# Ten seven-product units dealt evenly among the query/key tiles, with linear attention moved into the middle of the first stage

## The chip, the cores and the metric

The kernel runs on one core of a Trainium2 chip. The metric is the device time of one execution in microseconds (us), as a median over runs. Three runs of the kernel before gave 1986.81 us (1984.18 to 1990.47). The profile is of one further execution, which took 1983.73 us; its span, from the first to the last instruction, is 1981.9 us, so 1.83 us lie outside the span.

## The reference, cut to what matters

One layer of a hybrid model on 256 tokens of width 2048, all in float32. The input is multiplied by one wide matrix, and its product is cut into parts:

```python
parts = jnp.split(x @ w_in, cuts, axis=-1)      # 3 x (q, k, v) of 1024, gq, gk, gv, gr, g_low, m_a, m_b
# 3 groups of dilated attention, 8 heads of 128; mixed by a softmax over their log sums
ya = ya @ w_proj_a
log_a = log_sigmoid(g_low @ gla_gate_w + gla_gate_b) / 16
o = _gla(gq / 16, gk, gv, log_a)                # linear attention, 4 heads of 256 keys and 512 values
o = o * rsqrt(mean(o * o) + eps) * gla_norm_g
yb = (o * silu(gr)) @ w_proj_b
y = sigmoid(m_a) * ya + sigmoid(m_b) * yb
x = layernorm(alpha * x + y @ w_out)
x = layernorm(alpha * x + conv_ffn(x))          # 5632 wide, gated, with a 3-tap convolution
```

## The kernel before

**Two-part products.** Every weight is read once, in pieces of 128 x 2048 floats (1 MB). `split` (L135) makes of a piece a rounded high part on ScalarE (ACT, tile `whi`, L136) and the remainder on VectorE (DVE, tile `wlo`, L137), and TensorE (PE) multiplies high by high, high by low and low by high in a format that it takes at one pass. There are three buffers for `whi` and two for `wlo`. Raw pieces have buffers of two kinds: `raw`, two of them, and `quarter`, six. SyncE (SP) issues the loads in order of its queue; a load waits until a split has freed its buffer.

**Stage one** makes all that is multiplied out of `x`, in three shapes of work.

- A *tile* (`b16`, L219) is one piece with 128 output columns: 16 matmuls of 512 columns with `whi` (L212) and 16 of 256 columns with `wlo` (L214). 16 tiles make the linear attention's keys and queries (`gkq`, L501), and 48 make queries and keys of the 8 heads (`head`, L522).
- A *unit* (`seven`, L294) makes 1024 output columns by a seven-product scheme over quarters of the matrix, called A11 to A22 and B11 to B22 as usual: 8 loads into `quarter` buffers, and 7 products of 2 parts with 12 matmuls of 512 columns each (24 a product, L308). Its steps are `p1, p5, p67(0), p67(1), p3, p4, p2`. The products A, D, B, E take as weights sums of quarters: some are added by DVE (`add`, L321), others by a DMA that accumulates into the other quarter (`add_by_dma`, L324), which GpSimd (POOL) issues. `p67` adds `B22` into `T` by DVE and into `B12` by DMA; `p4` adds `B21` into `T` by DMA. The x side needs four sums of quarters of x, from `combine` (L273). 11 units are made: 3 for the heads' values (`v`), 4 for the output gates (`m`), 2 for the linear attention's values (`gv`), 2 for its gate (`gr`).
- *Side work* is a list of closures, `side`, from which `pump` (L173) takes one after each step and each tile: for each head a bias, three score blocks, two softmaxes, three transposes and three value products (`attend`, L421).

The order of the work (L554 to L577) is: two tiles, `combine`, and then the 63 steps of nine units (v, m, gv) with one tile after nearly every step. When the tiles are used up the low-rank gate input is made (L581 to L615), then the two `gr` units run with two closures after each step, among them `gate, decay, keys, att` and `outs` of the four heads of linear attention (`gla`, L624). Within a head these are a chain: a gate product (`pz`, L633) on PE, ACT functions and a running sum on DVE, decayed keys (`xk`, L652 to L684) on DVE, the products `patt` (L692) on PE, a mask on POOL (L700), and the products `pgo` (L710, L712) on PE. `drain()` (L730) makes the rest, and the pool `early` is closed. A scheduler orders the instructions of each engine, within what the buffers allow; the order of a program below is what it made.

**The other stages.** The heads' sums are loaded and split (L762 to L765) and multiplied by `w_proj_a` (`yp`, L792 to L798) while `gated_out` makes `ob`; then come `w_proj_b` (`pb`), `w_out` (`wo`), a layer norm, and the feed-forward part (`fg`, `fu`, `wd`). They use plain chunks (`a_chunk`, L248): for 512 output columns and 16 row blocks, four pieces with 24 matmuls of 512 columns each (L244 to L246). Their pieces come through the two `raw` buffers.

Of the kernel before, what the change touches and what calls it, by code (L numbers as in the profile page):

```python
# [17 lines left out]
P = 128  # L18
# [39 lines left out]
def hybrid_layer(ctx: ExitStack, tc: tile.TileContext, wp, xt, wgl, gw, par, relb, onehot, rows, xk, out):  # L58
# [80 lines left out]
    def raw_tile(i, tag="raw", bufs=2):  # L139
        return wpool.tile([P, 2048], F32, tag=tag, name=f"{tag}_{i}", bufs=bufs)  # L140
# [30 lines left out]
    side = []  # L171

    def pump(n=1):  # L173
        for _ in range(n):
            if side:
                side.pop(0)()

    def drain():
        while side:
            side.pop(0)()  # L180
# [92 lines left out]
    def combine(xs, raw):  # L273

        out = [res(f"comb{i}") for i in range(4)]
        for j in range(4):
# [11 lines left out]
        return out  # L288
# [5 lines left out]
    def seven(name, xs, comb, i, store):  # L294
# [48 lines left out]
        def p67(p):  # L343
            def f():
# [7 lines left out]
                add_by_dma(st["B12"][p], b)  # L352
# [68 lines left out]
    def attend(h, qk):  # L421
# [70 lines left out]
        return bias, [scores(g) for g in range(3)], [soft(0), soft(1), turn(0), turn(1), values, mix(0), turn(2), mix(1), mix(2)]  # L492
# [6 lines left out]
    tiles = []  # L499

# [13 lines left out]

    for which in range(2):
        for h in range(GH):
            f = gkq(which, h)
            first = not tiles
            tiles.append(f(0, [pair_of_x(j) for j in range(4)] if first else (None,)))
            tiles.append(f(1))  # L520
# [20 lines left out]
    for h in range(NH):  # L541
        tiles.extend(head(h))

# [10 lines left out]
    with tc.issue_after(loaded.ins):  # L554
        tiles.pop(0)()
    comb = []
    tiles.pop(0)()
    comb.extend(combine(X, XR))
    steps = []
    for g in range(3):  # L560
        steps.extend(seven("v", X, comb, AT["v", g], to_v(g)))
    for u in range(4):
        steps.extend(seven("m", X, comb, AT["m", u], to(M[u // 2], u % 2)))
    for u in range(2):
        steps.extend(seven("gv", X, comb, AT["gv", u], to(GV, u)))
    late = []
    for u in range(2):
        late.extend(seven("gr", X, comb, AT["gr", u], to(GR, u)))
    ratio = len(tiles) / len(steps)
    done = 0  # L570
    for n, step in enumerate(steps):
        step()
        pump()
        while done < (n + 1) * ratio and tiles:
            tiles.pop(0)()
            done += 1
            pump()  # L577

    glr = tmp("glr")  # L581
    nc.gpsimd.dma_start(glr, wgl)
    glh = tmp("glh", F32R)
    gll = tmp("gll", F32R)
    split(glh, gll, glr)


    places = [slice(r, r + RANK) for r in (0, 32, 64)]
    stack = slice(0, 64 + RANK)
    gws = []  # L590
    for j in range(2):
        w = blk("gws")
        nc.gpsimd.memset(w[stack], 0.0)
        for r in places:
            nc.gpsimd.dma_start(w[r], gw[:, j * 512 : (j + 1) * 512])
        gws.append(blk("gwp", F32R))
        nc.scalar.activation(gws[j][stack], w[stack], AF.Copy)
        r = places[1]
        nc.vector.tensor_tensor(gws[j][r], w[r], gws[j][r].bitcast(F32), op=ALU.subtract)
    gl = tmp("gl")  # L600
    nc.gpsimd.memset(gl[stack], 0.0)
    pg = bank("pgl")
    for kc in range(16):
        w = slice(kc * RANK, (kc + 1) * RANK)
        xo = xop(kc)
        nc.tensor.matmul(pg[:RANK], glh[:, w], xo, start=(kc == 0), stop=False)
        nc.tensor.matmul(pg[:RANK, S:], gll[:, w], xo[:, :S], start=False, stop=(kc == 15))
    nc.scalar.activation(gl[:RANK], pg[:RANK, :S], AF.Copy)
    nc.vector.tensor_tensor(gl[:RANK], pg[:RANK, S:], gl[:RANK], op=ALU.add)
    for r in places[1:]:  # L610
        nc.sync.dma_start(gl[r], gl[:RANK])
    glp = tmp("glp", F32R)
    nc.scalar.activation(glp[stack], gl[stack], AF.Copy)
    r = places[2]
    nc.vector.tensor_tensor(glp[r], gl[r], glp[r].bitcast(F32), op=ALU.subtract)  # L615

    O = [[] for _ in range(GH)]
    rmask = blk("rmask")
    nc.gpsimd.memset(rmask, 1.0)
    nc.gpsimd.memset(rmask.rearrange("p (c t) -> p c t", t=CH)[:, :, 0:1], 0.0)  # L620
    NG = blk("ng")
    nc.gpsimd.dma_start(NG, rows[4:5, :512].to_broadcast([P, 512]))

    def gla(h):  # L624
        st = {}

        def gate():
            pz = bank("pz")
            z = blk("gz")
            for j in range(2):  # L630
                dt = 2 * h + j
                c = slice(j * S, (j + 1) * S)
                nc.tensor.matmul(pz[:, c], gws[h // 2][stack, (dt % 4) * P : (dt % 4 + 1) * P], glp[stack], start=True, stop=True)  # L633
# [7 lines left out]
            nc.vector.tensor_tensor_scan(c, rmask, z, 0.0, op0=ALU.mult, op1=ALU.add)  # L641
            st["c"] = c

        def decay():
            c = st["c"]
# [59 lines left out]
        def outs():  # L705
            a = st["a"]
            gv = [fetch("gv", d) for d in GV[h]]
            for t in range(2):
# [10 lines left out]
                nc.vector.scalar_tensor_tensor(o, po, rs, NG, op0=ALU.mult, op1=ALU.mult)  # L719
                O[h].append(spill("os", o))  # L720

        return [gate, decay, keys, att], outs

    for h in range(GH):
        stages, o = gla(h)
        side.extend([*stages, o])
    for step in late:
        step()
        pump(2)
# [349 lines left out]
```

## Time and profile before

| | |
|---|---|
| median of 3 runs | 1986.81 us (1984.18 to 1990.47) |
| profiled execution | 1983.73 us, span 1981.9 us |
| PE busy | 1859.2 us, 94% of the span |
| DVE busy | 1333.7 us, 67% |
| ACT busy | 974.6 us, 49% |
| HBM read | 372.18 MB, 198 GB/s over the span |

How to read what the prediction quotes: the page's slices cut the span in 40 equal parts of 49.5 us, and each digit is the busy share in tenths; PEclk is the clock that TensorE was granted, in tenths of full speed. In rows by windows each engine has its busy time and, as (x...), the number of instructions, and then come the clock, the share of DMA engines that were busy and GB/s. In rows of the timeline the first two numbers are the start and the time in us; xN is how many instructions of a kind follow one another; in brackets stands the idle time of the engine before the row and what released it. In rows of the chain of waits there are the start, the time and what took it. In groups by line "a<-b" is output and input, xN the count, and after the bar come busy us and mean ns of one, then idle us before them.

### The profile page before, as it was taken

How to read it: one execution, taken by the hardware profiler on the slowest of the kernel's cores; microseconds unless marked ns; L12 is line 12 of the kernel's file. 1: busy time of each engine (PE TensorE's matmuls, PEld its weight loads, DVE VectorE, ACT ScalarE, POOL GpSimd, SP SyncE). 2: the span in 40 equal slices, each digit the busy share in tenths (PEclk: the TensorE clock that was granted, in tenths of full speed). 3: DMA queues.
4: the chain of work that ended last, by engine and by line, in shares of the span. 5: the costliest groups of instructions: out<-in, count | busy, mean ns of one | idle time of the engine just before them, and what ended most of it. 6: DMA issues, size and time to landing. Idle time of an engine off the chain costs nothing.

```text
span 1981.9 us, 23097 instructions
## 1 busy us (share of the span) xinstructions
PE 1859.2 (94%) x9246; PEld 1558.7 (79%) x9246; DVE 1333.7 (67%) x1181; ACT 974.6 (49%) x951; POOL 203.2 (10%) x305
## 2 busy tenths in 40 slices
PE   6889999999999999785699998899999999999996
PEld 4768888888888888663478886788888888888885
DVE  7667887878888788685375556766545666446657
ACT  5355555555546555465453334454434555335442
POOL 0100101110110111112320002400000000000001
PEclk9989999999999999887699999999999999999998
DMA  8689888887988978674386554555555555565553
GB/s 311 219 255 292 254 306 243 270 287 225 313 226 270 295 234 291 196 212 135 128 288 226 196 191 147 206 187 188 191 194 191 187 187 189 195 229 193 192 191 126
DMA packets 71927, 438.77 MB, mean 221 GB/s; under 512 B 9873, under 2 KB 10796, under 8 KB 24844
## 3 DMA queue, kind: packets, MB, share of 16 engines
q1 hardware_dynamic: 50316, 345.10, 47.9%
q0 software_dynamic: 21360, 91.95, 18.9%
q8 instruction: 72, 1.18, 0.2%
q14 instruction: 35, 0.29, 0.0%
q10 hardware_dynamic: 144, 0.26, 0.0%
HBM read 372.18 MB, written 20.09 MB: 198 GB/s over the span
## 4 chain that ended last, share of the span: by engine, by line
PE 82%; DMA 6%; DVE 6%; issue 3%; ACT 2%; POOL 1%; SPq 0%; ACTq 0%; POOLq 0%; DVEq 0%
PE qk L212 8%; PE fu L212 8%; PE fg L212 8%; PE qk L214 4%; PE fu L214 4%; PE fg L214 4%; PE wd_t L244 4%; PE wd_t L246 4%; PE wd_t L245 4%; DMA quarter<-quarter 3%; PE mA L308 2%; PE gqk L212 2%; DVE wlo L137 2%; PE mD L308 2%; PE mE L308 2%
## 5 line engine op out<-in xcount | busy, mean ns | idle before, releaser
L136 ACT ACTIVATE whi<-raw 128x2048 fp32r<-128x2048 f32 (+1 forms) x239 | 452.7, 1894 | 502.1 <-DMA raw<-in_wp 381.3
L137 DVE TENSOR_TENSOR wlo<-raw,whi 128x2048 fp32r<-128x2048 f32 (+1 forms) x239 | 544.7, 2279 | 213.2 <-PE wd_t L245 52.3
L137 DVE TENSOR_TENSOR wlo<-quarter,whi 128x2048 fp32r<-128x2048 f32 x154 | 351.8, 2287 | 151.5 <-ACT whi L136 125.2
L136 ACT ACTIVATE whi<-quarter 128x2048 fp32r<-128x2048 f32 x154 | 294.2, 1917 | 233.3 <-DMA quarter<-quarter 79.2
L212 PE MATMUL qk<-x,whi 128*128 128x512 f32 x768 | 188.6, 396 | 0.0
L212 PE MATMUL fu<-x,whi 128*128 128x512 f32 x688 | 166.1, 394 | 6.0 <-DVE yb L237 6.0
L212 PEld LDWEIGHTS qk<-x,whi 128*128 128x128 f32 x768 | 142.1, 188 | 28.5
L212 PE MATMUL fg<-x,whi 128*128 128x512 f32 x672 | 160.3, 391 | 2.0 <-ACT whi L136 2.0
L212 PEld LDWEIGHTS fu<-x,whi 128*128 128x128 f32 x688 | 127.6, 190 | 31.0 <-DVE yb L237 6.2
L212 PEld LDWEIGHTS fg<-x,whi 128*128 128x128 f32 x672 | 123.7, 188 | 26.3 <-ACT whi L136 2.2
L244 PE MATMUL wd_t<-whi,h 128*128 128x512 f32 x352 | 137.1, 390 | 0.0
L245 PE MATMUL wd_t<-wlo,h 128*128 128x512 f32 x352 | 137.0, 389 | 0.0
L246 PE MATMUL wd_t<-whi,h 128*128 128x512 f32 x352 | 136.9, 389 | 0.0
L214 PEld LDWEIGHTS qk<-x,wlo 128*128 128x128 f32 x768 | 98.6, 191 | 3.8
L321 DVE TENSOR_TENSOR quarter<-quarter,quarter 128x2048 f32<-128x2048 f32 x44 | 100.4, 2286 | 0.7
L214 PE MATMUL qk<-x,wlo 128*128 128x256 f32 x768 | 100.0, 283 | 0.0
L214 PEld LDWEIGHTS fu<-x,wlo 128*128 128x128 f32 x688 | 88.2, 191 | 3.3
L214 PE MATMUL fu<-x,wlo 128*128 128x256 f32 x688 | 89.2, 283 | 0.0
L214 PEld LDWEIGHTS fg<-x,wlo 128*128 128x128 f32 x672 | 86.2, 191 | 3.3
L214 PE MATMUL fg<-x,wlo 128*128 128x256 f32 x672 | 87.2, 283 | 0.0
L246 PEld LDWEIGHTS wd_t<-whi,h 128*128 128x128 f32 x352 | 66.1, 188 | 14.0 <-DVE h L137 0.2
L244 PEld LDWEIGHTS wd_t<-whi,h 128*128 128x128 f32 x352 | 66.1, 188 | 13.8 <-ACT h L136 0.5
(313 smaller groups left out, 2768.9 us busy)
## 6 DMA issues: line engine op xcount, KB each, us to landing
raw<-in_wp SPq DMA_DIRECT2D x235, 1024.0 KB, 5.0
quarter<-in_wp SPq DMA_DIRECT2D x88, 1024.0 KB, 7.2
quarter<-quarter POOLq DMA_DIRECT2D x44, 1024.0 KB, 8.5
sp<-c POOLq DMA_DIRECT2D x16, 256.0 KB, 4.1
m<-sp POOLq DMA_DIRECT2D x16, 256.0 KB, 5.3
row<-in_rows POOLq DMA_DIRECT2D x16, 256.0 KB, 3.9
bias<-bvd POOLq DMA_DIRECT2D x32, 96.0 KB, 9.8
v<-vs POOLq DMA_DIRECT2D x24, 128.0 KB, 8.5
```

Of the source, the lines that this page charges most:

```text
L136: nc.scalar.activation(hi, src, AF.Copy)
L137: nc.vector.tensor_tensor(lo, src, hi.bitcast(F32), op=ALU.subtract)
L212: nc.tensor.matmul(ps, parts(kc)[0], opnd(kc), start=(kc == 0), stop=False)
L214: nc.tensor.matmul(ps[:, S:], parts(kc)[1], opnd(kc)[:, :S], start=False, stop=(kc == nk - 1))
L244: nc.tensor.matmul(ps, xh, hi, start=first, stop=False)
L245: nc.tensor.matmul(ps, xh, lo, start=False, stop=False)
L246: nc.tensor.matmul(ps, xl, hi, start=False, stop=last)
L308: nc.tensor.matmul(ps, a(kc)[which], w[:, k * 512 : (k + 1) * 512], start=(first and w is hi and which == 0 and kc == 0), stop=(w is lo an ...
L321: tt(a, a, b, op=ALU.add)
```

## The change

1. **Start.** Four tiles come first instead of two, and `combine` is cut in four parts, of which two are called ahead of the third tile and two ahead of the fourth. The first unit (`v`, 0) makes all its sums by DVE (`by_dma=False`): four more 128 x 2048 additions on DVE, and four accumulating DMAs fewer.
2. **Ten units instead of eleven.** `m` has three units. The last 1024 columns of its second gate are two plain chunks (`a_chunk`, 8 pieces), at the end of stage one, with three closures after each piece.
3. **The order.** The steps of all ten units (v, gv, gr, m; 74 entries with four marks) and the rest of the tiles (65 entries) are dealt out evenly, so about six tiles stand among seven steps, and the units of `gr` no longer come last.
4. **Linear attention in the middle.** The low-rank part, the mask, the four gates and the norm's gain are put on the side list once the `gkq` tiles are done. Each head's running sum is written to DRAM and fetched again by `decay` (two DMAs of 256 KB more for each head, on POOL's queue). The stages `decay, keys, att, outs` of a head follow a head of dilated attention (after heads 1, 2, 3 and 4). A closure may carry a mark ("values", "gv"), and `pump` stops in front of it until the units that it needs are done.
5. **The end of stage one.** The splits of the heads' sums (`ya_parts`) are closures that run during the two plain chunks.
6. **Buffers.** From the end of stage one on, pieces are loaded into the six `quarter` buffers instead of the two `raw` buffers.

```diff
+    home = ["raw", 2]
+    def raw_tile(i, tag=None, bufs=None):
+        tag, bufs = (tag, bufs) if tag else home
...
     def pump(n=1):
         for _ in range(n):
             if side:
-                side.pop(0)()
+                mark, f = side[0] if isinstance(side[0], tuple) else (None, side[0])
+                if mark and mark not in passed:
+                    return
+                side.pop(0)
+                f()
...
-                add_by_dma(st["B12"][p], b)
+                (add_by_dma if by_dma else add)(st["B12"][p], b)
...
-                add_by_dma(a, b)
+                (add_by_dma if by_dma else add)(a, b)
...
-            st["c"] = c
+            DEC[h] = spill("gcs", c)
         def decay():
-            c = st["c"]
+            c = fetch("gc", DEC[h])
...
+    def head_tiles():
+        for h in range(NH):
+            yield from head(h)
+            if h in (1, 2, 3, 4):
+                yield lambda h=h: side.extend(gla_stages[h - 1])
+    def of_tiles():
+        yield from gkq_tiles()
+        yield lambda: side.extend([low_rank, start_mask, *gla_gates, norm_gain])
+        yield from head_tiles()
+    def by_unit(name, n, sink, mark=None):
+        for u in range(n):
+            yield from seven(name, X, comb, AT[name, u], sink(u), by_dma=(name, u) != ("v", 0))
+        yield lambda: passed.add(mark)
+    tiles = of_tiles()
+    with tc.issue_after(loaded.ins):
+        next(tiles)()
+    next(tiles)()
+    comb, part = combine(X, XR)
+    part(0)
+    part(1)
+    next(tiles)()
+    part(2)
+    part(3)
+    next(tiles)()
+    def of_units():
+        yield from by_unit("v", 3, to_v, "values")
+        yield from by_unit("gv", 2, lambda u: to(GV, u), "gv")
+        yield from by_unit("gr", 2, lambda u: to(GR, u))
+        yield from by_unit("m", 3, lambda u: to(M[u // 2], u % 2))
+    units = list(of_units())
+    rest = list(tiles)
+    done = 0
+    for n, step in enumerate(units):
         step()
-        pump(2)
+        pump()
+        while done < (n + 1) * len(rest) / len(units):
+            rest[done]()
+            done += 1
+            pump(2 if len(side) > 8 else 1)
+    side.extend(ya_parts(h) for h in range(NH))
+    for n in range(2):
+        pss = a_chunk("m", xop, 16, AT["mb"] + 4 * n, 3)
+        for t in range(2):
+            c = blk("mc")
+            nc.scalar.activation(c, pss[t], AF.Copy)
+            M[1][2 + n][t] = spill("ms", c)
     drain()
+    home[:] = "quarter", 6
```

Three places show what the scheduler made of it.

The first is VectorE at the start (`raw` and `quarter` are raw pieces, `comb` the sums of quarters of x, `gqk` the result of a tile). In the program before, the splits of the first unit's quarters stand directly behind the split of the second tile (`raw_196`), with the sums of `combine` around them:

```order
L137 TENSOR_TENSOR wlo_199<-raw_196,whi_198 128x2048
L237 TENSOR_TENSOR gqk_192<-gqk_159,pa_193 128x256
L137 TENSOR_TENSOR wlo_314<-quarter_308,whi_313 128x2048
L281 TENSOR_TENSOR comb_244<-xraw_115,xraw_137 128x256
L137 TENSOR_TENSOR wlo_330<-quarter_310,whi_329 128x2048
L237 TENSOR_TENSOR gqk_192<-gqk_202,pa_235 128x256
L282 TENSOR_TENSOR comb_245<-comb_244,xraw_115 128x256
```

In the changed program the third tile's split (`raw_276`) and then `combine` stand there:

```order
L137 TENSOR_TENSOR wlo_199<-raw_196,whi_198 128x2048
L246 TENSOR_TENSOR gqk_192<-gqk_159,pa_193 128x256
L137 TENSOR_TENSOR wlo_279<-raw_276,whi_278 128x2048
L291 TENSOR_TENSOR comb_244<-xraw_115,xraw_137 128x256
L246 TENSOR_TENSOR gqk_192<-gqk_202,pa_235 128x256
L292 TENSOR_TENSOR comb_245<-comb_244,xraw_115 128x256
```

So two more tiles come ahead of the first unit. Within that unit VectorE has more to do. Before, one addition of quarters stands at each half of `p67`, and none for `B12`; now there are two, the second of them for `B12` (`quarter_487`), here at `p67(0)`:

```order
L137 TENSOR_TENSOR wlo_534<-raw_531,whi_533 128x2048
L332 TENSOR_TENSOR quarter_395<-quarter_395,quarter_578 128x2048
L332 TENSOR_TENSOR quarter_487<-quarter_487,quarter_578 128x2048
L137 TENSOR_TENSOR wlo_582<-quarter_395,whi_581 128x2048
L246 TENSOR_TENSOR gqk_478<-gqk_537,pa_570 128x256
L137 TENSOR_TENSOR wlo_599<-quarter_487,whi_598 128x2048
```

Both additions stand ahead of the two splits of that step.

The second place is TensorE at the end of stage one. In the program before, the last heads of linear attention stand there alone (`pz` the gate, `patt` the decayed keys by the queries, `pgo` the result), and the first matmul of the next stage, `yp_t`, comes behind them:

```order
L633 MATMUL pz_6806<-glp_5936,gwp_5894 128x256 x2
L692 MATMUL patt_6844<-gq_6826,xk_6831 128x64 x4
L692 MATMUL patt_6844<-qx_6841,xk_6831 128x128 x2
L692 MATMUL patt_6844<-gq_6826,xk_6832 128x64 x4
L710 MATMUL pgo_6862<-gv_6858,att_6855 128x512
L710 MATMUL pgo_6874<-gv_6858,att_6855 128x512
L712 MATMUL pgo_6874<-gv_6860,att_6855 128x512
L244 MATMUL yp_t_864_6937<-whi_6941,ya_6897 128x512
```

In the changed program `patt` of the first such head stands within a query/key tile (`qk_3151`), with a product of a unit behind it:

```order
L223 MATMUL qk_3151<-x_85,wlo_3148 128x256 x3
L223 MATMUL qk_3151<-x_86,wlo_3148 128x256
L676 MATMUL patt_3131<-qx_3093,xk_3083 128x128 x2
L676 MATMUL patt_3131<-gq_3078,xk_3084 128x64 x4
L223 MATMUL qk_3151<-x_86,wlo_3148 128x256 x3
L319 MATMUL gvE_2940<-whi_3193,x_85 128x512 x8
```

And the first matmul of the next stage follows the last of the plain chunks (`m_t`):

```order
L255 MATMUL m_t_851_6784<-whi_6890,x_86 128x512
L253 MATMUL m_t_852_6785<-whi_6890,x_86 128x512
L254 MATMUL m_t_852_6785<-wlo_6891,x_86 128x512
L255 MATMUL m_t_852_6785<-whi_6890,x_86 128x512
L253 MATMUL yp_t_866_6942<-whi_6946,ya_6599 128x512
L254 MATMUL yp_t_866_6942<-wlo_6947,ya_6599 128x512
```

What stood alone on TensorE now has tiles and products on both sides.

The third place is TensorE between `p67(1)` and `p4` of the second `gv` unit. Before, a tile (`qk_5610`), the product `gvD` and a second tile (`qk_5700`) lie between the two; the rows are the end of the first tile, the product, two transposes and the beginning of the second tile:

```order
L214 MATMUL qk_5610<-x_86,wlo_5607 128x256 x4
L308 MATMUL gvD_5376<-whi_5653,comb_27_243 128x512 x8
L308 MATMUL gvD_5376<-wlo_5654,comb_27_243 128x512 x4
L308 MATMUL gvD_5376<-whi_5669,comb_27_243 128x512 x8
L308 MATMUL gvD_5376<-wlo_5670,comb_27_243 128x512 x4
L463 MATMUL ppt_5688<-ident,s_600_5456 128x128
L466 MATMUL ppt_5688<-ident,s_601_5457 128x128 x2
L212 MATMUL qk_5700<-x_83,whi_5696 128x512 x4
```

In the changed program the product stands inside the only tile (`qk_3151`), and the product of `p4`, `gvE` out of `x_85`, is the last row of the piece with `patt` above:

```order
L221 MATMUL qk_3151<-x_86,whi_3147 128x512 x4
L319 MATMUL gvD_2856<-whi_3096,comb_27_243 128x512 x8
L319 MATMUL gvD_2856<-wlo_3097,comb_27_243 128x512 x4
L319 MATMUL gvD_2856<-whi_3112,comb_27_243 128x512 x8
L319 MATMUL gvD_2856<-wlo_3113,comb_27_243 128x512 x4
L223 MATMUL qk_3151<-x_83,wlo_3148 128x256 x4
L223 MATMUL qk_3151<-x_84,wlo_3148 128x256 x2
```

So one tile fewer stands between the two steps in this unit. The same holds for the first `gr` unit; the other units keep two tiles there.

More of the change, by code (lines that the diff above doesn't have):

```diff
@@ L275, in combine, with part @@
         out = [res(f"comb{i}") for i in range(4)]
-        for j in range(4):
+        def part(j):
             n_blk[0] += 1
@@ L513, in gkq @@
         return f
[L515 to L520, printed above, removed]
     def head(h):
@@ L552, in to @@
         return f
[L554 to L611, printed above, removed]
```

104 lines of the change are left out of this document (73 added, 31 removed).

## The prediction

> **What bounds the kernel now.** I read the page first, then the chain of waits, then a table of busy time by windows whose edges I took from TensorE's timeline: its first tile, the end of the first unit, the last tile and product that are fed in rhythm, and the first matmul of the next stage. The page:
>
> ```profile
> span 1981.9 us, 23097 instructions
> ...
> PE 1859.2 (94%) x9246; PEld 1558.7 (79%) x9246; DVE 1333.7 (67%) x1181; ACT 974.6 (49%) x951; POOL 203.2 (10%) x305
> ...
> PE   6889999999999999785699998899999999999996
> ...
> PEclk9989999999999999887699999999999999999998
> ```
>
> PE is the bound nearly everywhere; slices 0 to 2 and 16 to 19 are the weak places, and there the clock drops too. The windows:
>
> ```profile
> 10.15:122.69 112.54, 86.82 (x403) 69.98 (x404) 77.67 (x81) 54.91 (x55) 9.25 (x14) 0.89 0.79 262
> 122.69:794.88 672.19, 671.45 (x3450) 569.46 (x3448) 537.92 (x390) 375.69 (x304) 89.60 (x137) 1.00 0.86 270
> 794.88:979.75 184.87, 127.19 (x460) 93.61 (x458) 110.40 (x110) 89.25 (x124) 35.64 (x59) 0.77 0.53 158
> 979.75:1982.00 1002.25, 971.02 (x4936) 825.26 (x4936) 606.22 (x598) 451.54 (x466) 67.16 (x87) 0.99 0.56 196
> ```
>
> From 122.69 to 794.88 PE idles 0.7 of 672 us at full clock, though DVE is busy 80% and the DMA engines 86%. So where tiles and products alternate, PE alone sets the pace, and the chain of waits gives that pace:
>
> ```profile
> 122.85 5.47 PE vA L308 x24
> 128.32 3.63 PE gqk L212 x16
> 133.86 5.47 PE vA L308 x24
> ```
>
> A product (24 matmuls) takes 5.47 us. From one product to the next with a tile between are 11.01 us, so a tile (32 matmuls) takes 5.54. The counts fit: 8 tiles and 6 products are 400 of the 403 matmuls in the first window.
>
> With these two prices, the first window holds 8 x 5.54 + 6 x 5.47 = 77.1 us of PE work and takes 112.5: **35.4 us are lost**. The third holds 13 products and little else, busy 127.19 us at clock 0.77, which is 97.9 us of full-clock work; it takes 184.87: **87.0 us are lost**. This is what the loss there looks like, in the list of waits and in PE's timeline:
>
> ```profile
> PE patt L692 <- DVE xk L668: 19.6, 3, 10.2
> PE pgo L710 <- POOL att L700: 5.6, 3, 3.4
> ...
> 941.51 1.97 PE L692 MATMUL patt<-gq,xk 128*128 128x64 f32 x8 [10.22 <-DVE xk L668]
> ...
> 961.39 1.97 PE L692 MATMUL patt<-gq,xk 128*128 128x64 f32 x8 [6.72 <-DVE xk L668]
> ...
> 979.75 0.80 PE L244 MATMUL yp_t<-whi,ya 128*128 128x512 f32 x1 [8.42 <-ACT ya L136]
> ```
>
> The chain of a head runs over five engines, and PE has nothing else to do; last it waits for the first split of the heads' sums. Now the start:
>
> ```profile
> 10.15 5.23 PE L212 MATMUL gqk<-x,whi 128*128 128x512 f32 x12 [4.28 <-ACT whi L136]
> ...
> 20.54 3.92 PE L212 MATMUL gqk<-x,whi 128*128 128x512 f32 x16 [0.69 <-ACT whi L136]
> ...
> 28.95 1.98 PE L308 MATMUL vA<-whi,x 128*128 128x512 f32 x8
> ...
> 44.05 3.78 PE L308 MATMUL vD<-whi,comb 128*128 128x512 f32 x8 [4.72 <-ACT whi L136]
> ...
> 107.19 3.79 PE L308 MATMUL vE<-whi,x 128*128 128x512 f32 x8 [14.65 <-ACT whi L136]
> ...
> 91.42 20.81 DMA quarter<-quarter
> ...
> 36.00:60.00 24.00, 16.82 (x79) 13.51 (x79) 24.00 (x27) 11.43 (x14) 1.79 (x2) 0.86 0.87 247
> ```
>
> The hole of 14.65 us ends an accumulating DMA of 20.81 us (`p4`), the one of 4.72 us follows `combine` on a DVE that is busy without a gap from 36 to 60. After both, eight matmuls took 3.78 us instead of 1.98: half clock.
>
> **The change, part by part.** The sum is made against the profiled execution, 1983.73 us.
>
> *Linear attention and the end of stage one: -87.0 us.* The PE work of the third window stays and is done elsewhere: the `gr` products in the rhythm of the second window, `patt` and `pgo` between tiles. The splits of the heads' sums lie under the plain chunks, so the wait of 8.42 us goes with the rest. What is late next is priced under new waits.
>
> *Start: 35.4 us lost become 13, -22.4 us.* DVE's prices are these, and a sum or split of `combine` is a quarter of the last row:
>
> ```profile
> L137 DVE TENSOR_TENSOR wlo<-quarter,whi 128x2048 fp32r<-128x2048 f32 x154 | 351.8, 2287 | 151.5 <-ACT whi L136 125.2
> ...
> L321 DVE TENSOR_TENSOR quarter<-quarter,quarter 128x2048 f32<-128x2048 f32 x44 | 100.4, 2286 | 0.7
> ...
> 38.04 1.41 DVE L137 TENSOR_TENSOR comb<-comb,comb 128x256 fp32r<-128x256 f32 x4
> ```
>
> The first tile takes 9.7 us (10.15 to its last matmul, with the loads of x), 4.2 over its price, and the second waits 0.7 as now. From 20.5 on DVE has to make 5 large splits (near 2.25 us each back to back), 25 pieces of `combine` and 3 small additions (0.35 each) up to the last split of `p1`: 21 us, to 41.5. PE comes to that split after three tiles and three quarters of a product, at 41.3. So `combine` is covered by the two tiles put ahead. From there to the second `p67` DVE has the rest of `combine`, 9 splits and 6 additions: 39 us, to 80.5. PE has 35 us of tiles and products in that time: it waits about 5. Together 4.2 + 0.7 + 5 = 10, and 3 for half clock behind the waits. The DMA hole of 14.65 us is gone, since the four DMAs of this unit are additions of 2.29 us. Bounds: 5 (no wait on DVE) and 35.4 (as now).
>
> Here a rule speaks against the edit. The Trainium skill ("Perfetto Trace Analysis", Optimizing Scalar/DVE Operations) says that work may be moved off a saturated DVE; the edit puts four additions onto it, and the row of 36 to 60 agrees that DVE is saturated there. By that rule 4 x 2.29 = 9.2 us would come on top of the 35.4, an estimate.
>
> *Ten units and two chunks: +5.5 us.* Seven products (7 x 5.47) go, eight pieces of 24 matmuls each come. DVE has 14 splits less and 8 more there, so the two `raw` buffers are enough: the feed-forward part of the last window is fed through them at PE's pace.
>
> *Clock at the next stage: -1.8 us.* Its first matmuls followed the 8.42 us of idleness:
>
> ```profile
> 982.26 0.43 PE yp_t L246
> ...
> 988.41 0.23 PE yp_t L246
> ```
>
> Nine of them stood 0.2 us too far apart; now a plain chunk runs right up to them.
>
> *Six buffers later: 0.* PE idles 31 us in the last window, and hardly ever for weights. One place could gain, at the layer norm:
>
> ```profile
> 1210.52 1.91 ACT L136 ACTIVATE whi<-raw 128x2048 fp32r<-128x2048 f32 x1 [3.64 <-DMA raw<-in_wp]
> ```
>
> The norm's functions stand behind this split, but their statistics come at the same time from DVE; between 0 and -3.6, I take 0.
>
> *New waits: +12 us.* (a) `p4` in two units. Now the second accumulating DMA starts about 14 us ahead of its use, and that is just enough:
>
> ```profile
> 256.44 0.98 POOL L324 DMA_DIRECT2D quarter<-quarter  x1 [11.02 <-DMA quarter<-in_wp]
> ...
> 270.79 1.98 PE L308 MATMUL vE<-whi,x 128*128 128x512 f32 x8
> ...
> quarter<-quarter POOLq DMA_DIRECT2D x44, 1024.0 KB, 8.5
> ...
> 175.45 13.83 DMA quarter<-quarter
> ...
> L136 ACT ACTIVATE whi<-quarter 128x2048 fp32r<-128x2048 f32 x154 | 294.2, 1917 | 233.3 <-DMA quarter<-quarter 79.2
> ```
>
> With one tile fewer 14.35 - 5.54 = 8.8 us are left. The DMA (8.5 to 13.8) and the split (1.9) need 10.4 to 15.7: 1.6 to 6.9 us are missing, I take 3 in the second `gv` unit and 3 in the first `gr` unit. Behind the waiting split on ACT stand the next splits and the results of tiles, so PE gets no other work. (b) Linear attention: `patt` and `pgo` waited 19.6 and 5.6 us for four heads with nothing between; now a tile or a product lies between the links. Ends 0 and 25.2, I take 1 a head, 4. (c) The low-rank part puts two small DMAs into SP's queue among the loads and an ACT copy behind them; a tile and a product of PE work cover them: 2. The running sums' eight DMAs on POOL cost nothing as long as the head before covers them. (d) The waits are mostly too short for the clock. A wait of 4.72 us cost 1.8 us of clock (3.78 less 1.98), so seven waits would cost at most 13; I take 0. The Trainium skill ("TensorE: Matmul & The Clock Gate", Part 1) has the clock halve after an idle window of about 3.4 us; the holes quoted agree, and a shorter one does so only in part:
>
> ```profile
> 824.09 0.79 PE L308 MATMUL grE<-whi,x 128*128 128x512 f32 x1 [2.55 <-ACT whi L136]
> ...
> 352.81 0.39 PE L308 MATMUL mE<-whi,x 128*128 128x512 f32 x1
> ```
>
> A matmul behind 2.55 us of idleness took twice as long, so the row says that (d) can be more than 0, where the rule says 0 for waits of this length.
>
> The sum: -87.0 - 22.4 + 5.5 - 1.8 + 12 = -93.7, that is 1890.0 us for the profiled execution. The median of the runs shown is 3.1 us above that execution, so the forecast is **1893 us**.
>
> **Rivals.** *VectorE becomes the bound.* In stage one it is busy 77.67 + 537.92 + 110.40 = 726 us now; six splits go (13.7), the additions by DMA that become additions replace those of the unit that goes: 712. If its share can't exceed the 0.80 of the second window, stage one takes 890 us from 10.15 on and ends at 900 instead of 979.75: 1983.7 - 79.6 - 1.8, 1905 by the median. At 0.78 it is 1928. For it: the 24 us without a gap, and that heads and linear attention now come together. Against: in the second window the 0.80 was PE's doing. The rule on a saturated DVE belongs here: with 44.6 us lost at the start the time would be 1893 + 31.6 = 1925. Chance 0.22.
>
> *No new waits.* The scheduler's order left 0.7 us idle in 672; if it does so with linear attention too, the 12 us go and 1881 is left; with 5 us lost at the start, 1873. Chance 0.16.
>
> *Slower: accumulating DMAs stop every unit.* Place: POOL's queue, where `p4`'s DMA may now stand behind the fetches and masks of linear attention, which wait for other engines. If each of the nine units that use DMAs had the hole of the first unit, 14.65 us and 1.8 for the clock, that is 148 us, and the time 1893 - 6 + 148 = 2035. It decides above (94 + 6) / 9 = 11 us a unit. Against: eight units of before had the same DMAs and no such hole. Chance 0.02.
>
> *The chain still stands alone*, if closures pile up behind marks and much of it runs at the end: half of the 87 us stay, 1936. Against: in the order `patt` of the first head stands amid the tiles. Chance 0.03.
>
> **How the numbers follow.** The forecast (1882 to 1904) has 0.57. The range takes in the rival without waits, 1873, and of the bound by VectorE all but its end, 1922; outside are the last two and the tail of that one, some 0.15. What a measurement here can't tell from no change is about 0.3%, 6 us. Only the slower rival and half as much for what I overlook end above that: faster 0.97, same 0.01, slower 0.02.
>
> **What would show it.** The first matmul of `yp_t` near 888 us, without a wait; PE near 100% and clock 1.00 from 100 us to there; the fourth slice no weaker than the fifth; no hole behind an accumulating DMA in the first unit, and DVE full until some 80 us; waits of `gvE` and `grE` for `whi` of a few us, one each; from `yp_t` to the end 1000 us as now (1002.25). I would be wrong if PE's idle time before `yp_t` were spread over all units (VectorE), or stood at `patt`, or if the second part of the kernel moved by more than 4 us.

## The result, and the profile after

The changed kernel takes 1942.74 us in the median of 4 runs (1941.12 to 1946.06), the kernel before 1986.82 (1984.18 to 1990.47): ratio 0.9779, with an interval of 0.9758 to 0.98. That is 44 us less, where 94 were forecast; the time lies above the range (1873 to 1922). Of the cases named beforehand the chain that still stands alone comes nearest, with 1936, but the profile shows something else.

First the page of the changed kernel (busy time by engine, then 40 slices of 48.5 us):

```profile
span 1939.2 us, 23074 instructions
...
PE 1850.2 (95%) x9270; PEld 1557.0 (80%) x9270; DVE 1316.5 (68%) x1170; ACT 961.0 (50%) x947; POOL 197.8 (10%) x305
...
PE   8999999979998989999999998899999999999997
...
PEclk9999999989999989999999998999999999999998
```

The weak slices 16 to 19 of before (counted from 0) are gone, and three single ones have come: 8, 12 and 14. The windows that go with them (length, then busy time of PE, PEld, DVE, ACT and POOL, clock, DMA share and GB/s), and the sum over the whole span:

```profile
10.09:102.66 92.57, 85.04 (x410) 69.38 (x411) 81.63 (x83) 49.41 (x53) 5.49 (x10) 0.96 0.67 251
102.66:190.00 87.34, 86.71 (x430) 72.97 (x431) 71.61 (x45) 51.94 (x36) 8.52 (x13) 1.00 0.93 310
190.00:260.00 70.00, 61.84 (x298) 48.80 (x297) 54.58 (x41) 41.29 (x45) 14.26 (x25) 0.98 0.73 216
...
400.00:440.00 40.00, 29.68 (x139) 25.39 (x138) 22.87 (x24) 18.02 (x17) 5.73 (x10) 0.83 0.79 239
440.00:505.00 65.00, 65.00 (x330) 54.42 (x330) 53.60 (x42) 36.95 (x39) 9.36 (x14) 1.00 0.78 245
...
600.00:660.00 60.00, 49.15 (x227) 39.84 (x226) 39.54 (x42) 27.13 (x34) 10.97 (x17) 0.89 0.69 225
660.00:700.00 40.00, 40.00 (x215) 34.56 (x214) 30.26 (x19) 22.96 (x18) 6.73 (x11) 1.00 0.82 262
700.00:730.00 30.00, 22.93 (x96) 18.40 (x95) 18.88 (x19) 16.44 (x24) 4.28 (x8) 0.83 0.82 285
730.00:890.00 160.00, 160.00 (x821) 135.95 (x821) 127.39 (x100) 88.25 (x73) 23.95 (x36) 1.00 0.88 272
890.00:939.20 49.20, 49.20 (x233) 40.67 (x233) 24.76 (x25) 24.42 (x29) 5.36 (x10) 1.00 0.49 172
939.20:1939.20 1000.00, 970.86 (x4938) 826.12 (x4936) 607.53 (x591) 451.39 (x462) 67.18 (x89) 0.98 0.55 194
sum 1939.20, PE 1850.22 PEld 1557.01 DVE 1316.52 ACT 961.01 POOL 197.78; mean PE 123.35 PEld 103.80 DVE 87.77 ACT 64.07 POOL 13.19
```

The first window holds nine tiles and five products, 77.2 us of work by the forecast's prices, in 92.6: 15.4 us are lost at the start, against 35.4 before. From the first `yp_t` to the end are 1000.0 us, against 1002.25. So the shortfall lies between: `yp_t` comes at 939.2 instead of 888. It isn't spread: from 730 to `yp_t` PE is never idle and at full clock, with DVE busy 80% up to 890. PE idles at the low-rank product and the gates (190 to 260), and at the four heads of linear attention (three shown; the second, 505 to 560, loses less). The waits there, first PE's, then those of DVE and ACT (in all, times, longest):

```profile
PE patt L676 <- DVE xk L652: 16.3, 2, 9.2
PE grE L319 <- DVE wlo L137: 8.6, 2, 5.4
PE pgo L696 <- DMA gv<-sp: 6.7, 2, 5.5
```

```profile
DVE gz L638 <- DMA gc<-gcs: 20.9, 3, 9.6
DVE gq L646 <- DMA gq<-gkqs: 9.9, 2, 8.6
ACT ge L631 <- DMA gc<-gcs: 20.1, 3, 10.9
```

PE waits for `patt` and for a weight split; but DVE and ACT, from which both come, wait themselves for fetches, DVE 30.8 us and ACT 20.1, in part at the same time: for a head's running sums (`gc`) and for its q and k (both `gq` in the rows). One such place, the third head, in the timelines of POOL, ACT, DVE and PE (start, duration, idle time ahead of it and what ended it):

```profile
590.13 0.86 POOL L335 DMA_DIRECT2D quarter<-quarter  x1 [12.27 <-DMA quarter<-in_wp]
...
592.34 0.55 POOL L114 DMA_DIRECT2D gc<-gcs  x1
...
605.74 0.63 ACT L631 ACTIVATE ge<-gc 128x512 f32<-128x512 f32 x1 [10.87 <-DMA gc<-gcs]
606.28 0.61 ACT L633 ACTIVATE ga<-gc 128x512 f32<-128x512 f32 x1
606.80 1.89 ACT L136 ACTIVATE whi<-quarter 128x2048 fp32r<-128x2048 f32 x1
...
605.74 0.69 DVE L638 TENSOR_TENSOR gz<-gc 128x512 f32<-128x512 f32 x1 [9.58 <-DMA gc<-gcs]
...
609.29 2.07 PE L319 MATMUL grE<-wlo,x 128*128 128x512 f32 x4 [5.36 <-DVE wlo L137]
```

POOL issues the 1 MB accumulating DMA of `p4` (`quarter<-quarter`) at 590.13 and the fetch 2.2 us behind it, with two smaller stores between. The fetch lands 13.4 us later. ACT and DVE stand at it, with the split that PE needs queued behind it on both. The four matmuls behind PE's wait then take 2.07 us, where four such take 1.07 at full clock. At all four heads the fetch of `gc` is issued 0.5 to 2.4 us behind an accumulating DMA of `p4`; it lands after 7.9 to 15.7 us, those of q and k after 8.9 to 14.5.

### The profile page after: what moved, and what is told of

Same layout as the page of the kernel before. It is cut to its first block, busy times and chain, and to the rows that moved or that the text cites. A ratio compares the mean times of both kernels' runs of the same rounds, so it can differ in the third digit from the quotient of the medians.

```text
span 1939.2 us, 23074 instructions
## 1 busy us (share of the span) xinstructions
PE 1850.2 (95%) x9270; PEld 1557.0 (80%) x9270; DVE 1316.5 (68%) x1170; ACT 961.0 (50%) x947; POOL 197.8 (10%) x305
## 4 chain that ended last, share of the span: by engine, by line
PE 79%; DMA 9%; DVE 7%; issue 3%; ACT 1%; POOL 1%; SPq 0%; POOLq 0%; DVEq 0%; ACTq 0%
PE fu L221 8%; PE fg L221 8%; PE qk L221 6%; PE fu L223 4%; PE fg L223 4%; PE wd_t L254 4%; PE wd_t L253 4%; PE wd_t L255 4%; PE qk L223 4%; DVE wlo L137 4%; DMA quarter<-quarter 2%; DMA quarter<-in_wp 2%; PE mA L319 2%; PE gqk L221 2%; PE wo_t L254 2%
## 5 line engine op out<-in xcount | busy, mean ns | idle before, releaser
L137 DVE TENSOR_TENSOR wlo<-quarter,whi 128x2048 fp32r<-128x2048 f32 x312 | 721.4, 2314 | 364.9 <-ACT whi L136 88.3
L136 ACT ACTIVATE whi<-quarter 128x2048 fp32r<-128x2048 f32 x312 | 597.0, 1916 | 498.2 <-PE wd_t L255 113.4
L137 DVE TENSOR_TENSOR wlo<-raw,whi 128x2048 fp32r<-128x2048 f32 (+1 forms) x75 | 165.1, 2201 | 37.1 <-ACT whi L136 12.5
L136 ACT ACTIVATE whi<-raw 128x2048 fp32r<-128x2048 f32 (+1 forms) x75 | 138.2, 1843 | 94.0 <-PE qk L221 42.9
L223 PE MATMUL qk<-x,wlo 128*128 128x256 f32 x768 | 104.4, 288 | 0.0
```

What stands on the lines that cost most here:

```text
L136: nc.scalar.activation(hi, src, AF.Copy)
L137: nc.vector.tensor_tensor(lo, src, hi.bitcast(F32), op=ALU.subtract)
L223: nc.tensor.matmul(ps[:, S:], parts(kc)[1], opnd(kc)[:, :S], start=False, stop=(kc == nk - 1))
```

## The experiments

The theory: a head's fetches are issued by POOL at the moment of use, right behind a 1 MB accumulating DMA, and land after 12 to 13 us in the median instead of some 4; DVE and ACT stand at them in order, the splits wait behind, PE runs dry and half its clock follows. The rivals: VectorE's load is the bound; the running sums' way through DRAM is the cost; the heads' chain of small operations is too long. Times are medians; ratios are to the kernel before, with their intervals, and the changed kernel's is 0.9779. The kernel before, run again beside each set, had medians of 1986.1 to 1989.0, so differences between sets can be off by some 3 us.

**Fetches earlier, eight closures.**

```diff
-            c = fetch("gc", DEC[h])
+            c = st["c"]
...
-        return gate, [decay, keys, att, ("gv", outs)]
+        return gate, early_qkc, [decay, ("gv", early_v), keys, att, outs]
...
-                yield lambda h=h: side.extend(gla_stages[h - 1])
+                yield lambda h=h: (side.insert(max(0, len(side) - 8), gla_early[h - 1]), side.extend(gla_stages[h - 1]))
```

> The changed kernel with one edit: each head's fetches of the running sums, q and k stand eight closures earlier in the queue of side work, and its two gv fetches two closures earlier, all still issued by POOL; nothing is left out. Theory (a head's fetches are issued right behind a 1 MB accumulating DMA of the same POOL queue, land after 12 to 13 us instead of 4, and DVE and ACT stand at them in order with the weight splits behind): the 32.8 us of PE idle at the four heads and some 10 of half clock behind it mostly go, 1942.7 becomes 1897 to 1913. Rival 1 (VectorE's load is the bound in the middle): the same work on DVE, 1937 to 1946. Rival 2 (the round trip of the running sums itself costs): it is still there, 1935 to 1945. Rival 3 (the heads' chain of small operations on DVE and ACT, not the fetch): 1930 to 1943.

Measured: 1901.1 us, ratio 0.9557 (0.953 to 0.9584). The DMA issues of this run (size, median time from issue to landing), its busy times, and its windows:

```profile
gq<-gkqs POOLq DMA_DIRECT2D x8, 256.0 KB, 3.7
...
gc<-gcs POOLq DMA_DIRECT2D x4, 256.0 KB, 3.4
```

```profile
PE 1840.5 (97%) x9270; PEld 1548.8 (81%) x9270; DVE 1316.1 (69%) x1170; ACT 960.6 (51%) x947; POOL 203.3 (11%) x305
```

```profile
400.00:430.00 30.00, 27.85 (x139) 23.37 (x138) 19.62 (x17) 13.55 (x12) 5.15 (x8) 0.98 1.02 319
...
590.00:630.00 40.00, 40.00 (x204) 33.35 (x203) 31.39 (x26) 22.29 (x28) 10.12 (x17) 1.00 0.88 269
630.00:680.00 50.00, 50.00 (x260) 42.75 (x259) 41.85 (x42) 32.71 (x32) 6.71 (x11) 1.00 0.89 292
...
sum 903.30, PE 872.21 PEld 725.01 DVE 709.96 ACT 509.06 POOL 135.45; mean PE 62.30 PEld 51.79 DVE 50.71 ACT 36.36 POOL 9.68
```

The fetches of `gc` and of q and k land in 3.4 and 3.7 us in the median, DVE and ACT no longer wait for one, and the heads pass with PE all but full. `yp_t` starts at 903.3, 35.9 us earlier. Up to there PE idles 903.3 - 872.2 = 31.1 us; in the changed kernel 939.2 - (1850.2 - 970.9) = 59.9. So 28.8 us of the 35.9 were idleness, and 7.1 were the same matmuls taking longer at the lower clock behind it. DVE's work is what it was (1316.1 and 1316.5 us), the running sums still go through DRAM, and the chain of small operations is whole: none of the rivals forecast this. Nor is DVE's share a bound at 0.80: from 630 to 680 it is 0.84 and PE is full.

**The gate back in its place.**

```diff
-            DEC[h] = spill("gcs", c)
+            st["c"] = c
...
-            c = fetch("gc", DEC[h])
+            c = st["c"]
...
-        return gate, [decay, keys, att, ("gv", outs)]
+        return [gate, decay, keys, att, ("gv", outs)]
```

> The changed kernel with the gate computed where it was before, ahead of each head's decay, and its running sum kept in SBUF: the four spills and four fetches of running sums go, q, k and gv are fetched as in the changed kernel; nothing is left out. Theory: the waits for gc (5.5, 9.6, 5.7 us on DVE) go, but q and k are still issued behind the accumulating DMA, so a part comes back there: 1918 to 1935. Rival 1 (VectorE): 1938 to 1945. Rival 2 (the round trip is the cost): all of it goes, 1895 to 1912. Rival 3 (chain of small operations): the chain is longer by the gate, 1943 to 1960.

Measured: 1933.61, 0.9733 (0.9699 to 0.9767): 9 us less, in the theory's interval. The trace, of an execution that took 1943.64 us, 10 above the median, bears out the theory's reason only at the first head: there q and k land after 12.0 to 13.5 us and `patt` waits 8.7. At the others they land after 3.9 to 9.4 us, and a new wait stands at the gate:

```profile
PE patt L676 <- DVE xk L652: 10.5, 2, 8.7
...
PE pz L617 <- ACT gz L618: 5.2, 1, 5.2
```

There ACT, whose copy of the gate PE needs, stands 6.1 us at a split of accumulated data. What the way through DRAM costs by itself is therefore not shown by this run; that it isn't what costs 41.6 us is shown by the one before, which keeps it.

**All additions by DVE.**

```diff
-            yield from seven(name, X, comb, AT[name, u], sink(u), by_dma=(name, u) != ("v", 0))
+            yield from seven(name, X, comb, AT[name, u], sink(u), by_dma=False)
```

> The changed kernel with the 36 accumulating DMAs of the other nine units made by DVE as in the first unit, so that POOL's queue has no 1 MB transfer; nothing is left out. 36 additions of 2.28 us are 82 us more on DVE. Theory: the fetches land in about 4 us, the heads' waits shrink by 20 to 35 us, and the load on DVE (80% in the stretch where PE is never idle, then some 90%) gives a part back: 1912 to 1940. Rival 1 (VectorE is the bound): 82 us more of its work makes it slower, 1965 to 2020. Rival 2 (the round trip): 1942 or slower. Rival 3 (chain of small operations): 1945 to 1965.

Measured: 1923.62, 0.9674 (0.965 to 0.9699), with this load and these landings:

```profile
PE 1850.5 (96%) x9270; PEld 1555.9 (81%) x9270; DVE 1389.9 (72%) x1206; ACT 961.0 (50%) x947; POOL 166.1 (9%) x269
...
gq<-gkqs POOLq DMA_DIRECT2D x8, 256.0 KB, 5.2
...
gc<-gcs POOLq DMA_DIRECT2D x4, 256.0 KB, 5.4
```

DVE does 73 us more and the kernel is 19 us faster. That refutes the rival of VectorE's load. How much of the gain is the fetches' is not shown: ACT's waits for accumulated data, 40.8 us in the changed kernel, go too, and its waits for DVE's sums grow from 52.7 to 77.9.

**Without the heads.**

```diff
-                yield lambda h=h: side.extend(gla_stages[h - 1])
+                yield lambda h=h: O.__setitem__(h - 1, GV[h - 1])
```

> The changed kernel without the four heads of linear attention: decay, keys, scores and outputs are left out, and the gating that follows reads gv in the place of their result; the low-rank product, the gates and their spills stay. It sizes what the four heads cost in all. Theory: PE's own work there (some 6 to 8 us a head) and 43 to 48 us of waits and half clock go: 1863 to 1878, with PE without a hole from 260 us on. Rival 1 (VectorE): its waits are spread over all units and heads take only 40 us of DVE's work, so 1895 to 1915.

Measured: 1889.78, 0.9499 (0.9472 to 0.9525). Both forecasts missed. The heads cost 53 us in all, where 65 to 80 were expected; 41.6 of them go with the earlier fetches alone, so some 11 are left. That isn't all of their own work. In the run with the earlier fetches PE spends 9.8 us on `patt` and 11.1 on `pgo`, some 5 a head, where 6 to 8 were expected; without the heads PE is busy 19.8 us less up to `yp_t` (852.4 against 872.2), but idles 4 us more (35.1 against 31.1), among others at the softmax attention:

```profile
PE ps L453 <- DVE qk L246: 5.8, 3, 2.4
...
PE ps L453 <- DVE s L455: 3.8, 3, 2.4
```

**Fetches by SP, at the old place.**

```diff
-            c = fetch("gc", DEC[h])
+            c = fetch("gc", DEC[h], by=nc.sync)
...
```

> The changed kernel with the fetches of the running sums, q, k and gv issued by SP, on its own queue, at the same places in the program's order; the accumulating DMAs stay on POOL. Theory (the delay is POOL's queue: the place behind the accumulating DMA): SP is not held by DVE or by that DMA, so the fetches are issued as soon as a buffer is free and land in about 5 us; most of what the earlier fetch gave is got without moving anything, 1900 to 1916. Rival (the fetch is asked for too late on any queue, its 4 us and the chain behind it are what costs): 1922 to 1940. Rival (SP then holds back weight loads behind a waiting fetch): 1940 or slower.

Measured: 1923.0, 0.9678 (0.9657 to 0.97), in the first rival's interval and not in the theory's: 20 us less, about half of what the earlier fetches give. So POOL's queue isn't the whole cause: on SP, whose queue carries the 1 MB weight loads, q and k land late too (the trace has the landing of only two of the eight, after 11.4 and 13.6 us):

```profile
gq<-gkqs SPq DMA_DIRECT2D x8, 256.0 KB, 12.5
```

Both were issued while an accumulating DMA of POOL's queue was under way, and until they landed the DMA engines were fully busy (share 1.02). So these runs don't separate the place in a queue from the large transfers that use the same DMA engines at that time. Busy engines alone made a fetch less late: in the changed kernel the `gv` fetch issued at 440.67, with no accumulating DMA under way, landed after 6.5 us at a share of 1.00.

**Fetches three closures earlier,** on POOL; the eight in the first experiment's edit becomes a three. Now they are asked for earlier, but stand right behind the second accumulating DMA of a step: of `p4` at three heads, of `p67(1)` at the first.

> The changed kernel with the fetches of each head three closures earlier instead of eight, so that they are asked for well ahead of their use but still stand right behind the two accumulating DMAs of p4 in POOL's queue; gv as in the run with eight. Theory A (what matters is the place behind the accumulating DMA, which makes them land after 12 to 13 us; three closures are some 8 to 16 us): the landing stays at 9 to 13 us, a part of the waits stays: 1905 to 1922. Theory B (what matters is only that they are asked for at the moment of use): all is got back, 1897 to 1905.

Measured: 1916.41, 0.964 (0.9615 to 0.9665), as theory A said. The landings and DVE's and ACT's waits:

```profile
gq<-gkqs POOLq DMA_DIRECT2D x8, 256.0 KB, 14.3
...
gc<-gcs POOLq DMA_DIRECT2D x4, 256.0 KB, 12.7
```

```profile
DVE gz L645 <- DMA gc<-gcs: 14.3, 3, 10.7
...
ACT ge L638 <- DMA gc<-gcs: 16.3, 3, 12.4
```

Behind the large DMAs the landing is late, and the lead covers only a part of it: `gc` is used 9.5 to 21.0 us after its issue, at three heads as soon as it lands. With eight closures it is used 29 to 53 us after. There the fourth head's fetches are also issued 3 to 4 us behind an accumulating DMA and land after 9.2 to 9.5 us, and nothing waits for them: a long enough lead does it without a better place.

**Fetches eight closures earlier, by SP** (the two edits together).

> The changed kernel with the fetches eight closures earlier and issued by SP. With the fetches early, the queue should no longer matter: 1896 to 1906, as with POOL (1901.1). If SP's queue costs by itself (fetches of the running sums, q, k and gv between the weight loads, SP waiting there for their buffers), 1910 to 1925, as with SP at the old place (1923.0).

Measured: 1899.61, 0.9557 (0.953 to 0.9583), the same as on POOL. Asked for early enough, the fetch costs nothing that these runs can show on either queue.

**The low-rank product in four closures,** with the earlier fetches.

```diff
-        yield lambda: side.extend([low_rank, start_mask, *gla_gates, norm_gain])
+        yield lambda: side.extend([low_loads, start_mask, norm_gain, low_split, low_rank, lambda: None, low_parts, *gla_gates])
```

> The run with earlier fetches by POOL (1901.1 us), and the low-rank product cut in four closures: its loads four closures ahead of its splits, the product, and its parts one closure after the copies; nothing is left out. Theory (between 190 and 260 us PE loses 8 to 10 us, standing at the low-rank product's loads and copies in order on ACT and DVE, as at the heads): 1890 to 1896. Rival (what is lost there is the load on ACT and DVE): 1898 to 1903.

Measured: 1897.12, 0.9555 (0.9538 to 0.9573): 4 us less than with the fetches alone, between the two forecasts, and by the ratios not to be told from it. The small holes between 190 and 260 us are gone, but a larger one stands at the gates (timelines of POOL, ACT and PE):

```profile
232.83 0.85 POOL L335 DMA_DIRECT2D quarter<-quarter  x1 [6.21 <-DVE c L369]
...
247.58 1.91 ACT L136 ACTIVATE whi<-quarter 128x2048 fp32r<-128x2048 f32 x1 [6.48 <-DMA quarter<-quarter]
249.40 0.46 ACT L631 ACTIVATE gz<-pz,prm 128x256 f32<-128x256 f32 x1
...
249.90 0.58 PE L630 MATMUL pz<-glp,gwp 80*128 80x256 f32 x1 [8.02 <-ACT gz L631]
```

ACT stands at a split of data that an accumulating DMA brings 14.7 us after its issue, and the gate's copy, for which PE waits, stands behind that split.

**That, and all three `v` units' additions by DVE.**

```diff
-            yield from seven(name, X, comb, AT[name, u], sink(u), by_dma=(name, u) != ("v", 0))
+            yield from seven(name, X, comb, AT[name, u], sink(u), by_dma=name != "v")
```

> The earlier fetches by POOL, the low-rank product in four closures, and all three v units' additions by DVE (24 of the 40 accumulating DMAs stay), since in the run with the four closures ACT stood 6.5 us at an accumulating DMA of the third v unit. Theory (that DMA, not the low-rank product's operations, is what still holds PE between 190 and 260 us): 8 us of wait and its half clock go, 1884 to 1892. Rival (DVE, with 8 additions or 18 us more, becomes late there): 1895 to 1905.

(The expectation miscounts: 28 accumulating DMAs stay.) Measured: 1887.78, 0.95 (0.9476 to 0.9523), as the theory said: 9 us less, and no wait of `pz` is left. From 190 to 260 us PE is now full, although DVE is busy 99% of that time:

```profile
190.00:260.00 70.00, 69.92 (x349) 56.95 (x348) 69.49 (x47) 46.45 (x45) 9.12 (x19) 1.00 0.59 204
```

It is the fastest version, 55 us below the changed kernel.

**The start alone,** on the kernel before: four tiles first, the combination in two halves between them, and the first unit's additions by DVE.

```diff
     tiles.pop(0)()
-    comb.extend(combine(X, XR))
+    comb, part = combine(X, XR)
+    part(0)
+    part(1)
+    tiles.pop(0)()
+    part(2)
+    part(3)
+    tiles.pop(0)()
...
-        steps.extend(seven("v", X, comb, AT["v", g], to_v(g)))
+        steps.extend(seven("v", X, comb, AT["v", g], to_v(g), by_dma=g > 0))
```

> The kernel before with the start of the change alone: four tiles ahead of the units instead of two, the combination in two halves between them, and the first unit's additions by DVE; nothing else moves. The prediction put this part at 22.4 us and the profile after shows some 20 of it (15.4 us lost at the start against 35.4). Theory (the start's gain reaches the end by itself): 1964 to 1969. Rival (part of it is given back at the later waits, as the units then run earlier against the same loads): 1972 to 1986.

Measured: 1970.92, 0.9917 (0.9902 to 0.9932): 15 us, between the two forecasts. The start itself saves what it saves in the changed kernel (the first row, of the same length as there), but the middle takes a part back, in a wait that the kernel before doesn't have, and `yp_t` comes 12.6 us earlier in its trace (967.1):

```profile
10.09:102.66 92.57, 84.52 (x410) 69.33 (x409) 80.78 (x83) 48.42 (x53) 5.49 (x10) 0.96 0.67 250
...
345.92 2.08 PE L310 MATMUL mE<-wlo,x 128*128 128x512 f32 x4 [4.81 <-DVE wlo L137]
```

The parts of the start (tiles, combination, additions) were not tried apart.

**Two buffers later, as before.**

```diff
-    home[:] = "quarter", 6
```

> The changed kernel with two buffers for the raw pieces after the first stage, as before, instead of six. The prediction put the six at 0 and the profile after shows 2.3 us less from the first yp on than before, of which 1.8 were put to the clock. Theory: 1941 to 1945. Rival (the six buffers carry those 2.3 us or more): 1945 to 1950.

Measured: 1950.59, 0.9821 (0.9806 to 0.9835): 8 us slower. Part of it is plain: from `yp_t` (944.7) to the end are 1005.9 us instead of 1000.0, with a hole that the changed kernel doesn't have, here in the list of waits and in the first window after `yp_t`; the last row is the same window of the changed kernel:

```profile
PE pt L799 <- ACT whi L136: 4.7, 1, 4.7
...
944.70:964.70 20.00, 15.32 (x61) 12.34 (x60) 9.89 (x8) 12.37 (x12) 8.70 (x19) 0.88 0.95 350
...
939.20:959.20 20.00, 20.00 (x93) 16.26 (x92) 13.79 (x12) 13.55 (x15) 10.83 (x23) 1.00 0.97 373
```

The other 5.5 us of its trace lie ahead of `yp_t`, where the edit changes nothing (PE waits 13.3 us at `grE` instead of 8.6). Why, stays open; a difference of this size in the waits of stage one can't be put down to an edit by one trace.

## Why the prediction was wrong

*The linear attention and the end of stage one (-87.0): right.* The third window with PE alone is gone: from 730 us to `yp_t` PE is full at full clock. What stands at the heads now is new waits.

*New waits (+12): the step that failed*, above all (b), "I take 1 a head, 4", and the sentence behind (c) that the running sums' eight DMAs "cost nothing as long as the head before covers them". Nothing covers the four fetches: each is asked for by the closure that uses it, whatever the head before does. The ends given for (b) were 0 and 25.2, from waits at `patt` and `pgo` alone; the earlier fetches are worth 41.6 us, because a fetch that DVE and ACT stand at holds up the splits of the tiles and products around it too, and the clock falls behind these waits. The forecast counted links of the chain between which PE has other work; it didn't ask what that work needs from DVE and ACT while these stand at a link. (c), put at 2, left something out as well: the low-rank product in four closures and the `v` units' additions by DVE are worth 13.3 us together, 9 of them in the step that took accumulating DMAs away, which no term had priced. (a), `p4` at 6, came out smaller: with the fetches out of the way PE waits 2.6 us for `gvE` and 1.0 for `grE`. (d), the clock at 0, was 7.1 up to `yp_t`, within the bound of 13: of the six waits of over 1.2 us at the heads five were of 3.3 to 9.2 us, not too short for the clock.

*The start (-22.4): sized nearly right at its place* (15.4 us lost instead of 13), in part by luck: of these PE idles 7.5 us where 10 were forecast, and the other 7.9, where 3 were put down to the clock, are matmuls that take longer than by the two prices. The 9.2 us that the four additions might have put on top did not come. Made alone the start is worth 15 at the end.

*The clock at `yp_t` and the six buffers (-1.8 and 0): right in sum* (-2.25), but not in the second part. With two buffers the earlier stage runs into a hole of 4.7 us, so the six aren't worth 0: by the one trace of each they keep 6 us from being lost.

The sum over what was measured: 41.6 for the heads instead of 4, 13.3 instead of 2, 3.6 for `p4` instead of 6 and 2.4 more at the start are 48.9 of the 49.7 us between forecast and result. The parts come from different runs and the 13.3 include an edit that the change doesn't have, so that the sum comes so near is partly chance. Not measured by itself: the ten units with two chunks (+5.5).

*The rivals.* VectorE as the bound (1905 to 1928) had the largest chance of the rivals, and is refuted: PE is full at DVE shares of 0.84 and 0.99, and 73 us more on DVE made the kernel faster. The slower rival named POOL's queue, but the wrong victim: not `p4` behind the fetches in every unit, but the fetches behind `p4`, four times. The chain that still stands alone has the nearest time, 1936, by accident: no part of the chain runs at the end. Of the signs of being wrong, idleness that "stood at `patt`" came, in part: 16.3 of the 59.9 us up to `yp_t`. The time from `yp_t` to the end came as forecast.

With the fetches early, the low-rank part spread and the `v` units' additions by DVE, the kernel takes 1887.8 us, near the 1893 forecast for the change. So most of the gain that was forecast is there to be had, though with an edit more than the forecast counted on, and what stood in its way was above all the change's own fetches.

## What to carry to other kernels

Moving a dependent chain between other work hides it only if no in-order engine has to stand at one of its links: ask for each link what is queued behind it on that engine, and who needs that. Where a spill is put into a chain, ask for its fetch well before its use, by more than it takes to land at that place, and better not right behind a large transfer: here a lead of three closures, behind one, got back 26 us, and a lead of eight closures 41.6. And price a fetch by its landing in that place, not by its median elsewhere in the trace.

## What the runs showed of the hardware

- The 256 KB fetches of running sums, q and k on POOL's queue landed in 3.1 to 4.3 us with no accumulating DMA under way (three heads of the first experiment), and in 7.9 to 15.7 us behind one (the changed kernel). Without any accumulating DMA on the queue, at the old place, their medians were 5.2 and 5.4 us. On SP, among the weight loads and with an accumulating DMA under way on POOL's queue, two landed after 11.4 and 13.6 us. The Trainium skill ("DMA: Bandwidth & Descriptors", Anatomy of one DMA — SWDGE (gpsimd) path) gives 2.0 us and the bytes at 436 GB/s for one DMA, an estimate of 2.6 us here. The shortest landings (3.1 us) are near it, and those behind an accumulating DMA are three to six times as long.
- Making 36 accumulating DMAs of 1 MB by DVE instead, 73 us of work for it, made the kernel faster by 19 us.
- PE lost clock as well as time at its waits: up to `yp_t` its work took 7.1 us longer than with the earlier fetches, a quarter of the 28.8 us of idleness itself. In the windows of the weak heads the granted clock was 0.83 to 0.89, in those without a wait 1.00.
- PE was full and at full clock for 70 us while DVE was busy 99% of them (the fastest version, 190 to 260 us).
